# Squares summed on TensorE by pairs of tiles, modulation a tile at a time, and a fixed instruction order at the beginning of a hybrid DeltaNet and neighbourhood-attention layer

## The chip, the cores and the metric

The kernel runs on one core of one Trainium2 chip. The metric is the device time of one execution in microseconds, taken as the median of three runs. The engines are named as in the profile: PE (TensorE, with PEld for its weight loads), DVE (VectorE), ACT (ScalarE), POOL (GpSimd) and SP (SyncE, which here only issues DMAs).

## The reference

One layer over 1024 latent tokens and 256 context tokens, width 1024. The part that the change touches is the very first step: the modulation vectors, the first RMSNorm, and the first column blocks of the input projection.

```python
mod_x = silu(c) @ w_ada + b_ada              # 6 x 1024 columns
mod_c = silu(c_ctx) @ w_ada + b_ada
sh1, sc1, ... = split(mod_x, 6);  csh1, csc1, ... = split(mod_c, 6)
px = (rms_norm(x,   norm1_w) * (1 + sc1)  + sh1)  @ w_in    # 1024 tokens
pc = (rms_norm(ctx, norm1_w) * (1 + csc1) + csh1) @ w_in    #  256 tokens
# rms_norm(x, w) = x * rsqrt(mean(x*x, over the 1024 features) + 1e-6) * w
...
# gated DeltaNet on 2064 columns, neighbourhood attention on 1536,
# output projection, gated residual, second norm, SwiGLU FFN, gated residual
```

## The kernel before

Activations lie transposed: 8 tiles `xt[k]` of 128 features by 1280 tokens (256 context tokens first, then 1024 latent ones). Products are made from float32 split in two parts, high and low, each in the TensorE's reduced form: for each tile `hh[k]` (high) and `hl[k]` (low) of the modulated activations, and `whi`, `wlo` of a weight block, three products are summed: hh with whi, hl with whi, hh with wlo. The 1280 tokens are cut into segments of 256, 512 and 512 columns (`SEGS`), so one block, one tile and one of the three products are three matmuls.

The beginning (lines 624 to 714) runs as follows. SP issues the loads: the 8 tiles of activations (640 KB each), the constants, 1 MB pieces of the modulation weights (`load_ada`, L630), the weights of the first two blocks (`fraw`, L641), six more pieces, and small tables. ACT squares each tile (L680), DVE adds the squares of tiles 0 to 6 into `acc` (L682), and PE multiplies `acc` and the last tile's squares by a matrix of ones (L687), which sums over the features and puts the sum on all partitions. ACT makes rs = exp(-0.5 * ln(mean + eps)) from it (L689 and L690, with a table load ahead of each).

The modulation for the tiles comes in four groups of two tiles. `ada(q)` multiplies the conditioning vectors (`wide`, 32 columns of which 2 count) by two 1 MB pieces (L662, 8 matmuls of 512 columns, each on a 32-row strip of the output), ACT copies the result to SBUF (`arow`, L665), and PE turns the rows into columns with the selector `sel` (L668, 4 matmuls of 2 columns). DVE adds the bias (`mod1`, L671) and makes the scale (`w1s`, L674). Then, for each tile k, DVE multiplies xt by the scale and rs (L701), ACT adds the shift and rounds to `hh` (L702), DVE makes `hl` (L704), each in a context part of 256 and a latent part of 1024 columns, and `b.mm([k])` (L397) issues the nine matmuls of each of the first two blocks. High and low weights of these two blocks are made by ACT (L193) and DVE (L194). Later blocks get their weights from SP's load (L192), ACT (L193) and POOL (L194), and their results are taken out of PSUM by ACT (L430) and run through the short convolution by DVE (L439). L207 loads the remaining modulation weights, which DVE sums in the background (L226, L228).

The order of instructions on each engine isn't the order of the source: a scheduler places each engine's instructions by its own estimate, under the dependences. Buffers come from pools; a buffer's next user waits for its last reader. `ascope` holds the modulation weights (seven buffers of 1 MB) and is closed ahead of tile 4, whose hh and hl reuse that memory.

Of the kernel before, what the change touches and what calls it, by code (L numbers as in the profile page):

```python
# [9 lines left out]
F32 = mybir.dt.float32  # L10
# [3 lines left out]
AF = mybir.ActivationFunctionType  # L14
OP = mybir.AluOpType
AX = mybir.AxisListType
# [4 lines left out]
KT = 8  # L21
# [31 lines left out]
WIN = (256, 0)  # L53
CTX = {256: slice(0, 256), 0: slice(384, 640)}
PACE = 0.72
ORDER = [list(range(NCH)), [1, 0] + list(range(9, 1, -1))]


# [29 lines left out]
def hybrid(ctx, tc, a, dbg):  # L88
# [15 lines left out]
    def lasting(name, shape, dt=F32):  # L104
        return persist.tile(shape, dt, name=name, tag=name)

    prm = lasting("prm", [128, 64])
# [17 lines left out]
    n1w, n2w, bada = prm[:, 0:8], prm[:, 8:16], prm[:, 16:64]  # L125
    cw = const("cw", [128, 12, 5])
    qkw = const("qkw", [128, 2])
    onw = const("onw", [128, 1])
# [52 lines left out]
            dve.scalar_tensor_tensor(r, y, 1.5, r, op0=OP.add, op1=OP.mult)  # L181

    def weights(wp, raws=2):
        def load(src, kt=KT, n=128, lo_engine=pool, raw=None):
# [8 lines left out]
            act.copy(h, r)  # L193
# [175 lines left out]
    with ExitStack() as bs:  # L369
# [13 lines left out]
        hh, hl = [], []  # L383
# [16 lines left out]
        class Block:  # L400
# [7 lines left out]
            def prefetch(self, raw=None, lo_engine=pool):  # L408
# [3 lines left out]
                self.w = load_w(src, lo_engine=lo_engine, raw=raw)  # L412

            def banks(self):
                self.pss = [(bank("blk"), s0, n) for s0, n in self.segs]
# [204 lines left out]
        with ExitStack() as xs:  # L620
            xp = pools(xs, "xp", "left")
            xt = []
            masks = xp.tile([128, 4, 128], F32, name="masks", tag="masks")
            ascope = ExitStack()
            wap = pools(ascope, "wap", "right", 7)
            aw = {}

            def load_ada(j):
                aw[j] = w = wap.tile([128, 4, 512], F32, name="wada", tag="wada")
                sp.dma_start(w, a["wa1"][j // 2, :, 4 * (j % 2):4 * (j % 2) + 4])  # L630

# [12 lines left out]
            sp.dma_start(cw, a["cw"])  # L644
            sp.dma_start(masks, a["masks"])
# [6 lines left out]
            sel = xp.tile([128, 2], F32, name="sel", tag="sel")  # L652
            rs = xp.tile([128, T], F32, name="rs", tag="rs")
            acc = xp.tile([128, T], F32, name="acc", tag="acc")

            def ada(q):

                p = bank("pm")
                for j in (2 * q, 2 * q + 1):
                    w = aw.pop(j)  # L660
                    for k in range(4):
                        pe.matmul(p[32 * k:32 * k + 32], wide[:, 4 * (j % 2) + k], w[:, k], start=j % 2 == 0,  # L662
                                  stop=j % 2 == 1)
                row = xp.tile([128, 512], F32, name="arow", tag="arow", bufs=2)
                act.copy(row, p)  # L665
                p = bank("pm")
                for b in range(4):
                    pe.matmul(p[:, 2 * b:2 * b + 2], row[:, b * 128:(b + 1) * 128], sel, start=True, stop=True)  # L668
                k = slice(2 * q, 2 * q + 2)
                m = mod1.rearrange("p (s b) c -> p s b c", s=2)[:, :, k]  # L670
                dve.tensor_tensor(m, p[:, 0:8].rearrange("p (s b c) -> p s b c", s=2, c=2),  # L671
                                  bada[:, 0:16].rearrange("p (s b c) -> p s b c", s=2, c=1)[:, :, k].to_broadcast(
                                      [128, 2, 2, 2]), OP.add)
                dve.scalar_tensor_tensor(w1s[:, k], m[:, 1], 1.0,  # L674
                                         n1w[:, k].rearrange("p (b c) -> p b c", c=1).to_broadcast([128, 2, 2]),
                                         op0=OP.add, op1=OP.mult)

            for k in range(KT):
                sq = xp.tile([128, T], F32, name="sq", tag="sq", bufs=2)
                act.activation(sq if k else acc, xt[k], AF.Square)  # L680
                if 0 < k < KT - 1:
                    dve.tensor_tensor(acc, acc, sq, OP.add)  # L682
            dve.tensor_reduce(sel, ident.rearrange("p (c i) -> p i c", i=32)[:, 0:2], AX.X, OP.add)
            sums = [bank() for _ in SEGS]
            for i, x in enumerate((acc, sq)):
                for p, (s0, n) in zip(sums, SEGS):
                    pe.matmul(p[:, :n], M[C_ONE], x[:, s0:s0 + n], start=i == 0, stop=i == 1)  # L687
            for p, (s0, n) in zip(sums, SEGS):
                act.activation(rs[:, s0:s0 + n], p[:, :n], AF.Ln, bias=b_eps, scale=1.0 / D)  # L689
            act.activation(rs, rs, AF.Exp, scale=-0.5)  # L690
            ada(0)
            for b, raw in zip(first, raws):
                b.prefetch(raw, dve)
            for k in range(KT):
                if k == 4:
                    ascope.close()
                    h_tiles(pools(bs, "hp2", "right"), 4)
                t = xt[k]
                parts = [(j, x, mod1[:, k, j:j + 1]) for j, x in ((1, slice(0, CT)), (0, slice(CT, T)))]
                for j, x, sh in parts:  # L700
                    dve.scalar_tensor_tensor(t[:, x], t[:, x], w1s[:, k, j:j + 1], rs[:, x], op0=OP.mult, op1=OP.mult)  # L701
                    act.activation(hh[k][:, x], t[:, x], AF.Identity, bias=sh)  # L702
                for j, x, sh in parts:
                    dve.scalar_tensor_tensor(hl[k][:, x], t[:, x], sh, hh[k][:, x].bitcast(F32),  # L704
                                             op0=OP.add, op1=OP.subtract)
                for b in first:
                    b.mm([k])
                if k < 3:
                    ada(k + 1)
                if k == 5:  # L710
                    act.copy(mr[:, 4], ident)
                    for d in range(2):
                        act.mul(mneg[:, d], masks[:, d], -1.0e30)
                    act.copy(mr[:, 0:4], masks)

        cp = pools(bs, "cp", "right")
        late = ExitStack()
# [903 lines left out]
def host(inputs):  # L1621
# [2 lines left out]
    o = {}  # L1624
    o["cst"], o["masks"] = const_arrays()
    o["c2"] = c(np.stack([f("c")[0].reshape(8, 128), f("c_ctx").reshape(8, 128)], -1).transpose(1, 0, 2))
    o["prm"] = c(np.concatenate([f("norm1_w")[0].reshape(8, 128), f("norm2_w")[0].reshape(8, 128),
                                 f("b_ada")[0].reshape(48, 128)], 0).T)
# [59 lines left out]
```

## Time and profile before

| what | value |
|---|---|
| median of 3 runs | 1605.53 us (1604.45 to 1607.15) |
| span of the profiled execution, first to last instruction | 1601.8 us |
| the profiled execution's own time | not recorded beyond the span; the median is 3.7 us above it |
| PE busy | 1509.9 us, 94% of the span |
| DVE busy | 1038.7 us, 65% |
| ACT busy | 706.1 us, 44% |
| POOL busy | 205.5 us, 13% |
| moved by DMA | 271.03 MB, mean 169 GB/s |

The page gives busy times by engine, and cuts the span into 40 slices of 40 us, so the beginning is the first slice and most of the second. The timeline view lists instructions in order of time: start, duration, engine, line, operation, output and inputs, shape, count, and in brackets how long the engine had been idle and what released it. A matmul's duration there includes its way through the array, so that neighbours overlap: the pace of a stream is read from start to start. A product of float32 numbers not split is shown as two rows for one matmul. The windows view gives each engine's busy time in a stretch, the clock that was granted to PE (1.00 is full; stretches for which nothing was recorded also show 1.00), the DMA share and the rate.

### The profile page before, as it was taken

To read this page: it belongs to the slowest core of one execution; us is meant where nothing else is said; L and a number is where in the kernel's file an instruction comes from. 1 tells how busy PE (TensorE), PEld (TensorE's weight loads), DVE (VectorE), ACT (ScalarE), POOL (GpSimd) and SP (SyncE) were. 2 spreads that over 40 slices of the span, in tenths; PEclk is the share of its full clock that TensorE was granted. 3 is DMA by queue.
4 is the path that set the end of the run, shared out by engine and by line. 5 is a ranking of instruction groups with operands and counts; after the bars stand their busy time and mean duration, and the time that the engine had idled before them with its cause. 6 is when DMAs were issued, how large, how long until landed. Compare 5 with 4: busy or idle time off the path is not lost. (4 is left out here: it accounts for less than half of the span.)

```text
span 1601.8 us, 24051 instructions
## 1 busy us (share of the span) xinstructions
PE 1509.9 (94%) x8626; PEld 1269.3 (79%) x8626; DVE 1038.7 (65%) x1934; ACT 706.1 (44%) x1341; POOL 205.5 (13%) x277
## 2 busy tenths in 40 slices
PE   4999999899898897999899999999999999999999
PEld 2788787679788786788777887888888888888887
DVE  4774496674364476667898648956665655679652
ACT  5342554553332325666674347333333333545441
POOL 0054401611333320011110000000000000000000
PEclk8999999999999999999999999999999999999999
DMA  9254222665345538999754910522333333698742
GB/s 387 63 190 133 71 74 78 202 200 178 117 150 184 182 102 228 311 286 288 217 161 135 310 55 27 197 99 99 112 101 107 116 109 109 233 369 299 254 153 85
DMA packets 206407, 271.03 MB, mean 169 GB/s; under 512 B 15952, under 2 KB 115792, under 8 KB 205264
## 3 DMA queue, kind: packets, MB, share of 16 engines
q1 hardware_dynamic: 200816, 264.73, 50.8%
q10 hardware_dynamic: 5472, 4.76, 0.9%
q8 instruction: 68, 1.11, 0.3%
q14 instruction: 51, 0.42, 0.1%
HBM read 204.68 MB, written 68.94 MB: 171 GB/s over the span
## 5 line engine op out<-in xcount | busy, mean ns | idle before, releaser
L397 PE MATMUL blk<-hh,whi 128*128 128x512 f32 (+1 forms) x416 | 125.1, 393 | 4.2 <-ACT hh L702 2.8
L1325 ACT CAST uhi<-ws 128x512 fp32r<-128x512 f32 x91 | 54.7, 622 | 153.8 <-PE ps L1264 75.1
L1325 ACT CAST uhi<-wq 128x512 fp32r<-128x512 f32 x101 | 60.3, 621 | 135.7 <-issue 61.3
L397 PE MATMUL blk<-hh,wlo 128*128 128x512 f32 (+1 forms) x416 | 117.8, 375 | 0.6 <-POOL wlo L194 0.6
L397 PE MATMUL blk<-hl,whi 128*128 128x512 f32 (+1 forms) x416 | 117.5, 374 | 0.0
L1326 DVE TENSOR_TENSOR ulo<-wq,uhi 128x512 fp32r<-128x512 f32 x101 | 67.2, 686 | 66.3 <-ACT uhi L1325 35.4
L1264 PE MATMUL ps<-hT,uhi 128*128 128x512 f32 x336 | 103.9, 390 | 3.1 <-ACT hT L1439 3.1
L1264 PE MATMUL ps<-lT,uhi 128*128 128x512 f32 x336 | 103.9, 391 | 0.0
L1264 PE MATMUL ps<-hT,ulo 128*128 128x512 f32 x336 | 103.8, 390 | 0.0
L1264 PE MATMUL ps<-hB,uhi 128*128 128x512 f32 x288 | 89.7, 392 | 0.0
L1264 PE MATMUL ps<-lB,uhi 128*128 128x512 f32 x288 | 89.2, 391 | 0.0
L1264 PE MATMUL ps<-hB,ulo 128*128 128x512 f32 x288 | 88.9, 389 | 0.0
L397 PEld LDWEIGHTS blk<-hh,whi 128*128 128x128 f32 x416 | 70.8, 194 | 19.7 <-issue 4.9
L397 PEld LDWEIGHTS blk<-hl,whi 128*128 128x128 f32 x416 | 73.5, 192 | 15.2 <-issue 1.7
L397 PEld LDWEIGHTS blk<-hh,wlo 128*128 128x128 f32 x416 | 73.3, 191 | 15.2 <-POOL wlo L194 0.9
L1326 DVE TENSOR_TENSOR ulo<-ws,uhi 128x512 fp32r<-128x512 f32 x91 | 60.7, 685 | 37.7 <-ACT uhi L1325 29.4
L580 PE MATMUL blk<-zhi,hh 128*128 128x256 f32 (+1 forms) x288 | 84.4, 293 | 0.0
L580 PE MATMUL blk<-zhi,hl 128*128 128x256 f32 (+1 forms) x288 | 82.9, 288 | 0.0
L580 PE MATMUL blk<-zlo,hh 128*128 128x256 f32 (+1 forms) x288 | 82.2, 285 | 0.0
L193 ACT CAST whi<-wraw 128x1024 fp32r<-128x1024 f32 x26 | 27.3, 1048 | 112.7 <-PE blk L397 55.7
L1264 PEld LDWEIGHTS ps<-hT,uhi 128*128 128x128 f32 x336 | 62.8, 188 | 16.5 <-ACT hT L1439 3.5
L1264 PEld LDWEIGHTS ps<-hT,ulo 128*128 128x128 f32 x336 | 63.4, 189 | 13.3
(352 smaller groups left out, 3749.0 us busy)
## 6 DMA issues: line engine op xcount, KB each, us to landing
wq<-w_fo SPq DMA_DIRECT2D x99, 256.0 KB
wq<-w_gu SPq DMA_DIRECT2D x88, 256.0 KB
wad<-wa SPq DMA_DIRECT2D x64, 256.0 KB
bt<-rpb SPq DMA_DIRECT2D x64, 192.0 KB
t_d<-g SPq DMA_DIRECT2D x22, 512.0 KB
fr<-t_d SPq DMA_DIRECT2D x44, 256.0 KB
f_d<-g SPq DMA_DIRECT2D x33, 256.0 KB
fr<-f_d SPq DMA_DIRECT2D x33, 256.0 KB
```

The costliest lines, as they stand in the source:

```text
L193: act.copy(h, r)
L397: pe.matmul(o, ww[:, k], xx[k][:, s], start=k == 0 and j == 0, stop=k == KT - 1 and j == 2)
L580: pe.matmul(p[:, :c1 - c0], x[k][:, s], ww[:, k, c0:c1], start=k == 0 and j == 0, stop=k == KT - 1 and j == 2)
L1264: pe.matmul(o, w[wi][:, k], x[xi][:, k], start=first and k == 0 and j == 0, stop=k == n - 1 and j == 2, skip_group_check=True)
L1325: act.copy(hi, self.raw[key])
L1326: dve.tensor_tensor(lo, self.raw[key], hi.bitcast(F32), OP.subtract)
```

## The change

The beginning is rewritten, from the loads to the end of the first two blocks; the later code is the same.

- **Loads**: the first blocks' weights come right behind the activations, then three pieces of modulation weights, the constants and masks, and the other five pieces. A piece now holds, for one tile, the shift and scale columns of all 8 feature groups (still 1 MB).
- **Squares**: ACT squares each tile, DVE adds two neighbouring tiles, and PE multiplies each sum of a pair by the ones as it comes, four times. The last pair goes by segments.
- **Modulation**: `ada(j)` and `column(j)` serve one tile (8 matmuls of 256 columns, 2 matmuls of 2), and stand apart: the table `AHEAD` says behind which tile and block each is issued. The selector comes from the host with `prm`.
- **Weights of the first blocks**: high and low parts of the first on DVE, of the second on POOL.
- **Tile 0** is normed by segments, and its products go in another order (both blocks' hh with whi, both hh with wlo, both hl with whi).
- **Order**: on PE, DVE and ACT this part keeps the order of the source (`manual_schedule`).

```diff
+AHEAD = {(1, 0): (3,), (1, 1): (3, 4), (2, 0): (4, 5), (2, 1): (5, 6, 7), (3, 0): (6, 7)}
...
-            act.copy(h, r)
+            if hi_engine:
+                hi_engine.tensor_copy(h, r)
+            else:
+                act.copy(h, r)
             lo_engine.tensor_tensor(o, r, h.bitcast(F32), OP.subtract)
...
-                aw[j] = w = wap.tile([128, 4, 512], F32, name="wada", tag="wada")
-                sp.dma_start(w, a["wa1"][j // 2, :, 4 * (j % 2):4 * (j % 2) + 4])
+                aw[j] = w = wap.tile([128, KT, 256], F32, name="wada", tag="wada")
+                sp.dma_start(w, a["wa1"][j])
...
-            sp.dma_start(cst, a["cst"])
             raws = [xp.tile([128, KT, 128], F32, name=f"fraw{i}", tag=f"fraw{i}") for i in range(2)]
-            for j in range(2):
-                load_ada(j)
             for i in range(2):
                 sp.dma_start(raws[i], a["w_conv"][4 + i])
-            for j in range(2, 8):
+            for j in range(3):
+                load_ada(j)
+            sp.dma_start(cst, a["cst"])
+            sp.dma_start(masks, a["masks"])
+            for j in range(3, KT):
                 load_ada(j)
...
+            def ada(j, copy):
+                p, w = bank("pm"), aw.pop(j)
+                for k in range(KT):
+                    s = slice(32 * (k % 4), 32 * (k % 4) + 32)
+                    pe.matmul(p[s, :256], wide[:, k], w[:, k], start=k < 4, stop=k >= 4)
+                rows[j] = xp.tile([128, 256], F32, name="arow", tag="arow", bufs=2)
+                copy(rows[j], p[:, :256])
+            def column(j):
+                p, row = bank("pm"), rows.pop(j)
+                for b in range(2):
+                    pe.matmul(p[:, 2 * b:2 * b + 2], row[:, b * 128:(b + 1) * 128], sel, start=True, stop=True)
...
+            with tc.manual_schedule(engines={mybir.EngineType.PE, mybir.EngineType.DVE, mybir.EngineType.Activation}):
+                sums = [bank() for _ in SEGS]
+                segs = [slice(s0, s0 + n) for s0, n in SEGS]
+                for k in range(0, KT, 2):
+                    sq = [xp.tile([128, T], F32, name="sq%d" % i, tag="sq%d" % i, bufs=2 + i) for i in range(2)]
+                    act.activation(sq[0], xt[k], AF.Square)
+                    for s in segs if k == KT - 2 else [slice(0, T)]:
+                        act.activation(sq[1][:, s], xt[k + 1][:, s], AF.Square)
+                        dve.tensor_tensor(sq[1][:, s], sq[0][:, s], sq[1][:, s], OP.add)
+                    for p, s in zip(sums, segs):
+                        pe.matmul(p[:, :s.stop - s.start], M[C_ONE], sq[1][:, s], start=k == 0, stop=k == KT - 2)
+                for p, s in zip(sums, segs):
+                    act.activation(rs[:, s], p[:, :s.stop - s.start], AF.Ln, bias=b_eps, scale=1.0 / D)
+                act.activation(rs, rs, AF.Exp, scale=-0.5)
+                first[0].prefetch(raws[0], dve, dve)
+                first[1].prefetch(raws[1], pool, pool)
+                ada(0, dve.tensor_copy)
+                column(0)
+                normed_tile(0, segs)
+                ada(1, act.copy)
+                for b in first:
+                    b.banks()
+                for j, (w, x) in enumerate(((0, hh), (1, hh), (0, hl))):
+                    for b in first:
+                        for o, s in b.outs:
+                            pe.matmul(o, b.w[w][:, 0], x[0][:, s], start=j == 0, stop=False)
+                        if j == 0 and b is first[1]:
+                            column(1)
+                            normed_tile(1)
+                ada(2, act.copy)
+                column(2)
+                for k in range(1, KT):
+                    if k == 3:
+                        ascope.close()
+                        h_tiles(pools(bs, "hp2", "right"), 4)
+                    if k + 1 < KT:
+                        normed_tile(k + 1)
+                    for j, b in enumerate(first):
+                        b.mm([k])
+                        for q in AHEAD.get((k, j), ()):
+                            if q in rows:
+                                column(q)
+                            else:
+                                ada(q, act.copy)
+                    if k == 5:
...
-    o["wa1"] = c(wada[:, :2048].reshape(8, 128, 2, 4, 256).transpose(3, 1, 0, 2, 4).reshape(4, 128, 8, 512))
+    o["wa1"] = c(wada[:, :2048].reshape(8, 128, 2, 8, 128).transpose(3, 1, 0, 2, 4).reshape(8, 128, 8, 256))
```

Each engine's order in the two built programs was compared. Behind the first two blocks it is the same on all engines but for a few places in the next blocks: PE takes some matmuls of the third and later blocks a few places earlier or later, DVE takes three background sums (L226, L228) behind the first convolution taps instead of ahead of them, and SP issues the next block's weights (L192) ahead of three background loads (L207) instead of behind them.

More of the change, by code (lines that the diff above doesn't have):

```diff
@@ L105, in lasting @@
         return persist.tile(shape, dt, name=name, tag=name)
-    prm = lasting("prm", [128, 64])
+    prm = lasting("prm", [128, 66])
     ones = lasting("ones", [128, 128])
@@ L124, in hybrid @@
     ident = M[C_ID]
-    n1w, n2w, bada = prm[:, 0:8], prm[:, 8:16], prm[:, 16:64]
+    n1w, n2w, bada, sel = prm[:, 0:8], prm[:, 8:16], prm[:, 16:64], prm[:, 64:66]
     cw = const("cw", [128, 12, 5])
@@ L183, in weights, with load @@
     def weights(wp, raws=2):
-        def load(src, kt=KT, n=128, lo_engine=pool, raw=None):
+        def load(src, kt=KT, n=128, lo_engine=pool, raw=None, hi_engine=None):
             given = raw is not None
@@ L651, in hybrid @@
             pool.tensor_copy(wide[:, :, 0:2], sc2)
-            sel = xp.tile([128, 2], F32, name="sel", tag="sel")
             rs = xp.tile([128, T], F32, name="rs", tag="rs")
[L654 to L697, printed above, removed]
+            rows = {}
+            def ada(j, copy):
[5 more added lines that the diff above has]
+                copy(rows[j], p[:, :256])
@@ L698, in hybrid, with normed_tile @@
+            def normed_tile(k, cuts=(slice(0, CT), slice(CT, T))):
                 t = xt[k]
-                parts = [(j, x, mod1[:, k, j:j + 1]) for j, x in ((1, slice(0, CT)), (0, slice(CT, T)))]
-                for j, x, sh in parts:
+                parts = [(x, mod1[:, k, int(x.start < CT):int(x.start < CT) + 1]) for x in cuts]
+                for x, sh in parts:
+                    j = int(x.start < CT)
                     dve.scalar_tensor_tensor(t[:, x], t[:, x], w1s[:, k, j:j + 1], rs[:, x], op0=OP.mult, op1=OP.mult)
@@ L702, in hybrid @@
                     act.activation(hh[k][:, x], t[:, x], AF.Identity, bias=sh)
-                for j, x, sh in parts:
+                for x, sh in parts:
                     dve.scalar_tensor_tensor(hl[k][:, x], t[:, x], sh, hh[k][:, x].bitcast(F32),
                                              op0=OP.add, op1=OP.subtract)
-                for b in first:
[L707 to L714, printed above, removed]
+            with tc.manual_schedule(engines={mybir.EngineType.PE, mybir.EngineType.DVE, mybir.EngineType.Activation}):
[18 more added lines that the diff above has]
+                ada(1, act.copy)
+                for b in first:
+                    b.banks()
[22 more added lines that the diff above has]
+                    if k == 5:
+                        act.copy(mr[:, 4], ident)
+                        for d in range(2):
+                            act.mul(mneg[:, d], masks[:, d], -1.0e30)
+                        act.copy(mr[:, 0:4], masks)
```

13 lines of the change are left out of this document (9 added, 4 removed).

## The prediction

> **What bounds the kernel now.** I read the page first, then the stretches of the beginning, then its timeline and the waits.
>
> ```profile
> span 1601.8 us, 24051 instructions
> ...
> PE   4999999899898897999899999999999999999999
> ...
> PE 39%; DVE 1%; ACT 1%; issue 0%
> ```
>
> The span is PE's: full in nearly all slices, and nearly all of the chain that ended last. That chain covers only 41% of the span, so it doesn't reach back to the beginning, but the row of PE has its one large hole there: slice 1, the first 40 us, is at 4 tenths.
>
> ```profile
> 10.00:15.00 5.00, 0.00 (x0) 0.00 (x0) 4.64 (x4) 3.82 (x3) 0.00 (x0) 1.00 1.02 415
> ...
> 26.00:33.00 7.00, 2.66 (x16) 1.78 (x8) 2.48 (x5) 4.97 (x6) 0.00 (x0) 0.76 1.01 421
> 33.00:40.00 7.00, 5.59 (x13) 3.03 (x13) 6.18 (x8) 2.91 (x4) 0.00 (x0) 0.50 1.02 395
> 40.00:50.00 10.00, 10.00 (x64) 5.93 (x64) 4.85 (x9) 2.90 (x5) 0.00 (x0) 1.00 0.17 41
> ...
> 74.00:100.00 26.00, 25.42 (x144) 21.80 (x143) 20.19 (x31) 14.37 (x22) 10.71 (x5) 1.00 0.45 149
> 100.00:140.00 40.00, 40.00 (x313) 37.98 (x312) 19.58 (x26) 15.93 (x38) 22.53 (x29) 1.00 0.60 191
> ```
>
> Behind each stretch and its length stand the busy times of PE, PEld, DVE, ACT and POOL with their instructions, then PE's clock, the DMA share and GB/s. In the last three rows PE is full but for 0.6 us. Before that it is idle, or (33 to 40) at half clock. Loads run at 415 GB/s.
>
> ```profile
> 7.06 1.27 ACT L680 ACTIVATE sq<-xt 128x1280 f32<-128x1280 f32 x1 [0.17 <-DMA xt<-xcT]
> ...
> 16.60 1.27 ACT L680 ACTIVATE sq<-xt 128x1280 f32<-128x1280 f32 x1 [0.29 <-DMA xt<-xcT]
> ...
> 17.94 4.64 PE L687 MATMUL m<-acc,ones 128*128 128x256 f32 x6 [17.94 <-DVE acc L682]
> ...
> 22.37 2.57 PE L687 MATMUL m<-sq,ones 128*128 128x256 f32 x6
> ...
> 24.87 1.92 PE L662 MATMUL pm<-wada,wide 128*32 128x512 f32 x16
> 24.98 0.69 ACT L689 ACTIVATE rs<-m,bias 128x512 f32<-128x512 f32 x1 [0.17 <-PE m L687]
> 25.56 1.03 ACT L193 CAST whi<-fraw 128x1024 fp32r<-128x1024 f32 x1
> ...
> 26.61 1.28 ACT L690 ACT_TABLE_LOAD   x1
> ...
> 27.91 1.27 ACT L690 ACTIVATE rs<-rs 128x1280 f32<-128x1280 f32 x1
> ...
> 29.70 1.87 PE L668 MATMUL pm<-sel,arow 128*128 128x2 f32 x8 [2.91 <-ACT arow L665]
> ...
> 32.60 0.51 ACT L702 ACTIVATE hh<-xt,mod 128x256 fp32r<-128x256 f32 x1 [2.00 <-DVE xt L701]
> 33.16 0.58 PE L397 MATMUL blk<-hh,whi 128*128 128x256 f32 x1 [1.59 <-ACT hh L702]
> ```
>
> This is the chain of the beginning: last tile at 16.6, sums on PE, logarithm, exponential (done at 29.18), modulation of the first tiles, first product at 33.16.
>
> ```profile
> 74.21 0.75 PE L397 MATMUL blk<-hl,whi 128*128 128x256 f32 x3
> ...
> 74.79 0.75 PE L397 MATMUL blk<-hh,wlo 128*128 128x256 f32 x3
> ...
> 75.38 0.51 PE L397 MATMUL blk<-hh,whi 128*128 128x256 f32 x2
> ```
>
> Three matmuls of 256, 512 and 512 columns take 0.585 us from start to start, and at 75.38 groups of two begin: the third block. So the first two blocks end at **75.38**, and the question is when they end now.
>
> **The change, step 1: rs.** The sum moves under the loads. Pair one can be added when the second tile is squared (7.06 + 1.27 = 8.33).
>
> ```profile
> L682 DVE TENSOR_TENSOR acc<-acc,sq 128x1280 f32<-128x1280 f32 x6 | 8.9, 1492 | 7.9 <-ACT sq L680 7.5
> ```
>
> Adding takes 1.49, so PE starts at about 9.9. It now sums four times instead of twice. The same three matmuls took 22.37 - 17.94 = 4.43 us from rest and 24.87 - 22.37 = 2.50 after that, so I take 4.43 + 3 x 2.50 = 11.9: done at 21.8 instead of 24.87. The last third of the last pair is there at about 19.1 (16.60, 1.7 for squaring in three cuts, 0.7 for the last addition), before PE asks for it at 19.3, so PE sets this, not the loads. Then ACT: 0.1 to start, 0.69, table load 1.28, exponential 1.27: rs at **25.2** instead of 29.18. The rounding of weights that stood in between (1.03) goes to DVE and POOL.
>
> **Step 2: the first product.** Before, 3.98 us lay between rs and it (copy of the row, the 1.87 for the selector, bias and scale, xt, hh). Now tile 0's columns are made ahead of rs. Its piece lands at about 21.7 (16.6, then twice 0.5 MB and 1 MB at 415 GB/s); `ada(0)` is half of 1.92, the copy some 0.4 by DVE, the selector half of 1.87, bias and scale 0.4: 24.6, just under the cover of ACT's exponential. If a load is 1 us late, 0.4 of it shows. What remains is xt (0.48) and hh (0.51) and the crossings: first product at **26.3**, 6.9 earlier. This half of the gain is nearly certain if step 1 holds.
>
> **Step 3: the two blocks.** PE's own floor: 8 tiles x 2 blocks x 3 products x 0.585 = 28.1; `ada` 1 to 7, one of which lies ahead of 26.3, is 6 x 0.96 = 5.8; seven `column` calls.
>
> ```profile
> 44.61 1.01 PE L668 MATMUL pm<-sel,arow 128*128 128x2 f32 x8
> ...
> 45.66 0.17 DVE L671 TENSOR_TENSOR mod<-pm,prm 128x8 f32<-128x8 f32 x1 [5.08 <-PE pm L668]
> 45.85 0.16 DVE L674 SCALAR_TENSOR_TENSOR w1s<-mod,prm 128x4 f32<-128x4 f32 x1
> ```
>
> Four selector matmuls take 1.01 at full clock, so two take 0.5, seven times 3.5: 26.3 + 28.1 + 5.8 + 3.5 = 63.7. Both kinds are the same total work as before, cut finer; DVE's small operations double (0.4 us for each tile with the hand-overs). But in source order DVE is slower than that.
>
> ```profile
> 65.44 1.68 DVE L701 SCALAR_TENSOR_TENSOR xt<-xt,w1s,rs 128x256 f32<-128x256 f32 x2
> ...
> 67.03 0.48 DVE L704 SCALAR_TENSOR_TENSOR hl<-xt,mod,hh 128x256 fp32r<-128x256 f32 x1
> 67.15 1.15 ACT L702 ACTIVATE hh<-xt,mod 128x1024 fp32r<-128x1024 f32 x1 [0.69 <-DVE xt L701]
> ...
> 68.33 1.29 DVE L704 SCALAR_TENSOR_TENSOR hl<-xt,mod,hh 128x1024 fp32r<-128x1024 f32 x1 [0.82 <-ACT hh L702]
> ```
>
> This is one tile on its own: xt, xt, hl, a wait of 0.82 for ACT, hl, 4.1 us until DVE can begin the next. The scheduler filled that wait with the next tile's xt; the fixed order can't, and pays it eight times. DVE then needs 25.2 + 8 x 4.1 + 7 x 0.4 = 60.8. To this come waits for the columns of tiles 1 and 2, which are not issued ahead: ACT copies their rows only behind hh of the tile before, and PE has products of both blocks queued in front. Tile 1's row is copied at about 28.3 and its column made at about 29.8, while DVE is free at 28.7 (25.2 and 3.5 for tile 0), with bias and scale a wait of 1.5; tile 2's comes up to 1 late in the same way. So the last hl is ready at 63.3, and five of PE's six products of tile 7 (2.9) follow it: **66.2**. Masks and constants on ACT (1.5 us between tiles 6 and 7) lie in DVE's time. At full clock throughout the waits for columns shrink by 1.7: 64.5. If PE runs from 26 to 33 us at half clock, as it did from 33 to 40 before, it does 3.3 us less in that time: 67.8. I take 66.3: 75.4 - 66.3 = **9.1 us**.
>
> Half clock is the point to weigh. The windows above grant 0.50 from 33 to 40, although PE worked in most of it, after a stretch (26 to 33) with 2.66 busy of 7. The new beginning has such a stretch too, from the sums' end to about 30. The Trainium skill ("TensorE: Matmul & The Clock Gate", Part 1) says that PE's clock is halved after a window of some 3.4 us with little work and restored after a busy one. The rows agree as to both directions. By that rule the result would be the 67.8 (7.6 us gained), inside my range.
>
> The second block's weights now pass through POOL beside DVE's work.
>
> ```profile
> 88.81 2.46 POOL L573 TENSOR_TENSOR zlo<-wraw,zhi 128x1056 fp32r<-128x1056 f32 x1 [4.58 <-DVE acc L228]
> ...
> 89.38 3.23 DVE L228 SCALAR_TENSOR_TENSOR acc<-wad,sc,acc 128x512 f32<-128x512 f32 x2
> ```
>
> The first of these two DVE operations begins inside POOL's and the pair takes 3.23, though neither waited for data: a DVE operation can be held up by a whole POOL one. The weights land at 19.1; a copy of at most 2.5 and a subtraction of 2.46, taking turns with DVE's two, end at about 24.5, ahead of xt at 25.2. If they collide, up to 2.4 us are lost; I take 0. The Trainium skill ("SBUF — State Buffer", "Who interferes with whom") gives the reason, a port pair that DVE and POOL take turns on; this row agrees.
>
> **Step 4: does the gain reach the end?** The instruction order behind the two blocks is the same but for a few neighbours.
>
> ```profile
> PE pr L928 <- DVE y L938: 7.2, 4, 4.0
> PE pr L928 <- DVE kk L919: 6.9, 11, 2.1
> PE sc L296 <- DVE mx L298: 5.7, 5, 4.2
> ...
> SPq L207 <- ACT mr L714: 20.4, 1, 20.4
> ```
>
> PE's later waits are for DVE, ACT and POOL, whose work hangs on the same blocks; the first later load waits for ACT's copy of the masks, which moves forward too. The three background sums that DVE did in its idle time before the first convolution (2 us) now stand between its taps; PE is behind with other blocks then, so 0, at most 2. I carry all 9.1 over: span 1592.7, and with the 3.7 us by which the median stands above the span, **1596.4**, said as 1596.5.
>
> **The rivals.**
>
> *Cold sums.* Every pair at 4.43: rs 5.8 later, and the end at 72.1: 1602.2. For it: PE pauses between pairs once it is fast. Against: each sum at the slow pace is longer than the loads of a pair (3.2 us), so PE doesn't pause while it is slow; in the old trace the pace rose under just this work.
>
> *Given back later.* The beginning is 9 us shorter, but the blocks behind meet something that didn't move (a load, POOL's backlog) or more half-clock stretches: 1604, no difference. Against: PE is full from 74 to 140, and no load stands at the top of PE's waits.
>
> *Columns in line (slower).* In fixed order a tile's path may close into a ring: `ada` 0.96, row copy 0.4, selector 0.5, bias and scale 0.4, DVE's 4.1 and hand-overs, 6.6 a tile instead of 4.5, more at half clock (another 0.5). It decides if tiles 3 to 7 wait for their columns as I let 1 and 2. Then seven times 2.1 to 2.6, less the 2.5 counted, are 12 to 16 us on 66.3: 78.5 to 82, some 3 to 7 us behind the old 75.4: about 1610. Against: columns 3 to 7 are issued one to three tiles ahead.
>
> *Better.* Full clock, no waits for columns: PE's floor 63.7 or slightly less: 1593.
>
> **How the numbers follow.** 0.2%, about what a measurement of this kernel can tell from no change, is 3.2 us: faster is below 1602.3, slower above 1608.7. Chances: forecast (1594 to 1599.5) 0.68, better 0.07, cold sums 0.10 (half of it counted as faster), given back 0.09, columns in line 0.06. So faster 0.80, same 0.14, slower 0.06. The range 1593.0 to 1602.5 holds the forecast, most of the better case and the cold sums.
>
> **What would show it.** The new trace should have sums from 9.9 to 21 or 22, the exponential's end near 25, the first product near 26.3, groups of two (third block) near 66, DVE with waits of 0.8 for ACT in each tile 3 to 7, and no PE wait for a column from tile 3 on. I am wrong if rs comes after 27, if the third block starts after 70, or if it starts at 66 and the end doesn't move by about as much.

## The result and the profile after

The changed kernel takes **1618.68 us** (median of 4 runs, 1615.66 to 1619.54) against 1605.84 for the kernel before beside it: ratio **1.0074**, 95% interval 1.0060 to 1.0088. It is 12.8 us slower, where 9 us faster was forecast. The profiled execution has a span of 1617.0 us against 1601.8.

The page of the changed kernel, the rows that answer to those of before:

```profile
span 1617.0 us, 24224 instructions
...
PE   6999898999888898999899999999999999999999
...
PE 40%; DVE 1%; ACT 1%; issue 0%
```

The hole of the first 40 us is partly filled (6 tenths instead of 4), and PE is full elsewhere, as before. The stretches of the beginning, with the columns as before (PE, PEld, DVE, ACT, POOL, clock, DMA share, GB/s):

```profile
10.00:15.00 5.00, 4.79 (x7) 2.52 (x8) 1.75 (x3) 4.03 (x4) 0.00 (x0) 1.00 1.02 423
26.00:33.00 7.00, 6.29 (x18) 4.94 (x19) 5.29 (x10) 2.83 (x6) 0.00 (x0) 0.53 1.03 431
33.00:40.00 7.00, 6.51 (x56) 4.15 (x55) 4.09 (x8) 3.13 (x5) 0.00 (x0) 0.99 0.98 382
40.00:50.00 10.00, 10.00 (x101) 7.14 (x100) 6.94 (x13) 2.68 (x5) 0.00 (x0) 1.00 0.16 42
74.00:100.00 26.00, 26.00 (x152) 22.58 (x151) 20.82 (x33) 13.11 (x19) 13.43 (x10) 1.00 0.58 192
100.00:140.00 40.00, 38.07 (x311) 36.58 (x310) 16.34 (x24) 16.84 (x42) 17.88 (x23) 1.00 0.62 197
```

PE works from 10 us on, and the half clock lies at 26 to 33 us instead of 30 to 40. From the timeline of the changed kernel, the sums, the exponential, the first product and the first group of two (the third block):

```profile
10.21 11.78 PE L700 MATMUL m<-sq,ones 128*128 128x256 f32 x24 [10.21 <-DVE sq L698]
...
24.03 1.27 ACT L703 ACTIVATE rs<-rs 128x1280 f32<-128x1280 f32 x1
...
26.42 0.58 PE L715 MATMUL blk<-hh,whi 128*128 128x256 f32 x1 [1.21 <-ACT hh L685]
...
69.07 0.51 PE L401 MATMUL blk<-hh,whi 128*128 128x256 f32 x2
```

So rs is done at 25.30 (before 29.18), the first product comes at 26.42 (33.16) and the third block at 69.07 (75.38). The beginning did gain, 6.3 us here. To see where it went, I paired each matmul with the same one of before and took the difference of their starts: -6.9 us at 70, -5.4 at 200, -3.5 at 510, 0.0 from 700 to 900, **+0.6 at 1000 and +14.9 at 1590**. Two losses, then: 7.5 us between 70 and 1000, in steps, and 14.3 us at an even rate from 1000 on, in the FFN, which the change does not touch. The windows show that second one. Before, then after:

```profile
1000.00:1300.00 300.00, 300.00 (x1332) 248.62 (x1331) 191.60 (x304) 106.99 (x193) 0.00 (x0) 1.00 0.35 117
```

```profile
1000.00:1300.00 300.00, 300.00 (x1296) 242.60 (x1295) 187.68 (x297) 104.93 (x189) 0.00 (x0) 1.00 0.33 115
```

PE is busy without a gap in both and has its full clock, but it gets through 36 matmuls fewer in 300 us. No wait, no DMA, no clock: each matmul takes longer. The timeline, before and after:

```profile
1200.18 0.62 PE L1264 MATMUL ps<-hB,uhi 128*128 128x512 f32 x2
1200.63 0.62 PE L1264 MATMUL ps<-lB,uhi 128*128 128x512 f32 x2
...
1202.45 0.61 PE L1264 MATMUL ps<-hT,ulo 128*128 128x512 f32 x2
1202.90 0.62 PE L1264 MATMUL ps<-hT,uhi 128*128 128x512 f32 x2
```

```profile
1200.40 0.63 PE L1288 MATMUL ps<-hT,uhi 128*128 128x512 f32 x2
1200.87 0.63 PE L1288 MATMUL ps<-lT,uhi 128*128 128x512 f32 x2
...
1203.19 0.61 PE L1288 MATMUL ps<-hB,uhi 128*128 128x512 f32 x2
1203.64 0.62 PE L1288 MATMUL ps<-lB,uhi 128*128 128x512 f32 x2
```

From start to start a pair takes 0.45 us before, 0.47 after with `hT`; and in the changed kernel some pairs with `hB` still take 0.45. Over single matmuls the median is 227 ns before and 234 to 235 after for `hT` and `lT`. An engine that is 100% busy in both profiles hides this: only a count, or start to start, shows it.

What differs is one line of the diff that the section on the change mentions in a clause (the selector comes from the host with `prm`):

```diff
-    prm = lasting("prm", [128, 64])
+    prm = lasting("prm", [128, 66])
```

`prm` is the first tile of the left-side memory, and its 256 bytes a partition become 288 with padding, so every later left-side tile stands 32 bytes further on. Tiles allocated from the right side don't move. In the FFN the weights `uhi`, `ulo` are left tiles, of the moving operands only `hB11` and `lB11` are; `hT`, `lT` and the other `hB`, `lB` are right ones. In the compiled programs (bytes in a partition):

```
                       before  changed  prm 80  pad 64
uhi   (weights)         24800    24832   24864   25056
hB11  (moving, left)    49632    49664   49696   49888
hT1   (moving, right)  180192   180192  180192  180192
uhi - hT1, modulo 256       0       32      64       0
```

Of the FFN's 2796 matmuls of 512 columns (2795 intervals from start to start), 2268 have their distance changed; the 528 with `hB11` and `lB11` keep it, and those are the pairs that still take 0.45 us. In this one execution the mean from start to start is 227.4 ns over the matmuls that stand at distance 0 and 233.3 over those at 32. The kernel has pads in front of the FFN's pools (`shift(ctx, "pad", "left", 8)`, L1249 of before), with which all of them stand at distance 0 before.

### The profile page after: what moved, and what is told of

Read it like the earlier page. It is cut to its first block, busy times and chain, and to the rows that moved or that the text cites. A ratio compares the mean times of both kernels' runs of the same rounds, so it can differ in the third digit from the quotient of the medians.

```text
span 1617.0 us, 24224 instructions
## 1 busy us (share of the span) xinstructions
PE 1531.6 (95%) x8702; PEld 1275.3 (79%) x8702; DVE 1037.6 (64%) x1944; ACT 704.8 (44%) x1345; POOL 209.8 (13%) x279
## 5 line engine op out<-in xcount | busy, mean ns | idle before, releaser
L1350 DVE TENSOR_TENSOR ulo<-wq,uhi 128x512 fp32r<-128x512 f32 x101 | 67.3, 689 | 68.3 <-PE ps L1631 29.9
L1288 PEld LDWEIGHTS ps<-lT,uhi 128*128 128x128 f32 x336 | 63.4, 189 | 15.4
```

Source lines behind the costliest of these rows:

```text
L1288: pe.matmul(o, w[wi][:, k], x[xi][:, k], start=first and k == 0 and j == 0, stop=k == n - 1 and j == 2, skip_group_check=True)
L1350: dve.tensor_tensor(lo, self.raw[key], hi.bitcast(F32), OP.subtract)
```

## The experiments

**Theory**: the distance between weights and moving operand sets the pace of the FFN's matmuls, and the 32 bytes cost the 14 us. **Rivals**: the new order, the clock, or the DMA makes the FFN slow; or the loss is the half clock's.

### The 32 bytes alone, in the old kernel

```diff
-    prm = lasting("prm", [128, 64])
+    prm = lasting("prm", [128, 72])
-    act.dma_start(prm, a["prm"])
+    act.dma_start(prm[:, 0:64], a["prm"])
```

> The kernel before the change with nothing but prm 72 columns wide instead of 64 (the load fills the first 64): the 32-byte shift alone, with the old beginning. Address theory: the FFN pace goes from 227 to 234 ns and the time from 1605.8 to 1619-1621, slower than the changed kernel by about the 0 to 6 us that its beginning gains. Rival (order or clock): nothing changes, 1605-1607.

Measured: 1621.36 us, ratio 1.0109 (1.0089 to 1.0128) to the kernel before; 16.3 us slower with not one instruction of the computation changed. The median pace of the `hT` products is 234 ns, and the same matmul falls behind by 14.3 us from 1000 to 1590, as in the changed kernel. That shows the cause of the larger loss; order and beginning are not needed for it.

### 64 bytes instead of 32, in two ways

```diff
-    prm = lasting("prm", [128, 66])
+    prm = lasting("prm", [128, 80])
-    act.dma_start(prm, a["prm"])
+    act.dma_start(prm[:, 0:66], a["prm"])
```

> The changed kernel with prm 80 columns wide instead of 66 (the load fills the first 66), so that every later tile of the left-side pools moves by another 32 bytes and stands in 64-byte steps where it stood before the change. Address theory: the FFN's 512-column matmuls go back from 234 to 227 ns start to start; over some 2,900 of them that is about 14 to 18 us, and the time falls from 1618.7 to 1600-1605. Rival (the slower FFN comes from the new order or the clock): pace stays at 234 and the time at 1617-1620. A third possibility: the pace hangs on 128- or 256-byte steps, which this does not restore; then too it stays at 1617-1620.

```diff
-    shift(ctx, "pad", "left", 8)
+    shift(ctx, "pad", "left", 16)
```

> The changed kernel with prm left at 66 columns and the left-side pad ahead of the FFN's pools 16 instead of 8 wide: only the FFN's left tiles are moved by 32 bytes, those of the blocks before it stay shifted. Address theory: FFN pace 227 ns, time 1600-1605; if the slow loss of the gain between 250 and 680 us comes from the shift as well, this one is 4-6 us slower than the kernel with prm 80 wide; if that loss comes from half-clock stretches, the two agree within 2 us. Rival (order or clock): 1617-1620.

Measured: 1613.92 (ratio 1.0058, 1.0043 to 1.0073) and 1614.15 (1.0054, 1.0039 to 1.0069). The pace stays at 233 ns and the loss from 1000 to 1590 at 14.4 and 14.3 us. My first guess, steps of 64 bytes, fell. The two agree within 0.3 us, so it makes no difference whether the tiles ahead of the FFN stand 64 bytes further on (the first) or 32 (the second). What 32 against 0 does there is seen in two runs of the old kernel: from 80 to 1000 us the one with `prm` 72 wide, whose tiles are moved there, falls 3.5 us behind the first profile of before, and the one with the pad 56 wide (below), whose tiles are not, 2.9 us. So the addresses cost little ahead of the FFN, as far as single profiles show it.

### The distance by itself

A program of nothing but 512-column matmuls in groups of 12, with the start of the weights moved by 32 bytes from group to group, for five starts of the moving operand. It leaves out the whole computation.

> A program of nothing but 512-column fp32r matmuls (it leaves out the whole computation and writes one product as output): groups of 12 with two weight tiles in turn, a group for each of 17 starts of the weights, 32 bytes apart, and 5 starts of the moving operand (0, 32, 64, 128, 256 bytes on); finer steps of 8 bytes; and groups with one weight tile for two matmuls, as in the blocks. Address theory: groups come at 227 or 234 ns start to start, and which of them is decided by the distance of weights and moving operand within 128 bytes (0 is fast) or within 256. Rival 1: each operand's own start decides (one row or one column of the table is fast throughout). Rival 2: all groups are alike at one pace, and the pace in the whole kernels hangs on something that this program does not have (DMA, other engines' reading).

Each entry is the mean of ten intervals from start to start within a group, in ns; the columns are the weights' start, the rows the moving operand's:

```
bytes      0    32    64    96   128   160   192   224   256
  0    226.6 233.1 233.3 234.0 231.7 233.8 229.2 233.1 226.6
 64    229.0 233.2 226.7 233.1 233.3 234.0 231.6 233.7 229.2
128    231.7 233.7 229.2 233.1 226.6 233.1 233.3 234.0 231.7
256    226.6 233.1 233.3 234.0 231.7 233.8 229.2 233.1 226.6
```

Each row is the one above, moved along: for starts that are multiples of 32 bytes neither operand's own start counts, only weights minus moving operand, modulo 256 bytes. 0 is fast, 192 costs 2.6 ns, 128 costs 5.1, the others 6.5 to 7.4. The row for 32 bytes follows it too, but for its first group at distance 0, which came at 229.0: there the single intervals are 235, 225, 230, 236, 229, 232, 231, and 227 only from the eighth on. With one weight tile for two matmuls in turn the values are the same, but for such a first group at each start (230.5 and 228.9). Finer steps of the weights, with the moving operand at 0, give 230.7 ns at 8 bytes and 233.2 at 16. With the moving operand itself at 16 bytes the rule does not hold: the weights at 16 too (distance 0) give 231.1, and the least, 228.4, comes with the weights at 48. All this was measured in one execution. There is no DMA and no other engine's work in that stretch, so those rivals are out.

### The table used on the whole kernel: 192 bytes, and back to 0

```diff
-    shift(ctx, "pad", "left", 8)
+    shift(ctx, "pad", "left", 56)
```

This edit is made in the kernel before:

> The kernel before the change with that pad 56 instead of 8 wide, 192 bytes: the FFN's weights then begin 192 bytes (modulo 256) from the moving operands for 2268 of the 2795 matmuls. The table of offsets gives 229.2 ns there, 2.6 more than at 0: 2268 x 2.6 = 5.9 us, 1611. If only in line or not in line counts (a step, not the table's values), as with prm 72 wide: 1619-1621. If the distance doesn't matter: 1605.

Measured: 1612.09, ratio 1.0031 (1.0018 to 1.0043), 5.4 us slower where the table gave 5.9; the same matmul loses 5.6 us from 1000 to 1590. It is the table's value, not a step.

```diff
-    shift(ctx, "pad", "left", 8)
+    shift(ctx, "pad", "left", 64)
```

This one is made in the changed kernel (32 and 224 more bytes make 256):

> The changed kernel with the left-side pad ahead of the FFN's pools 64 instead of 8 wide: with prm's 32 bytes that makes 256, so weights and moving operands of the FFN begin a multiple of 256 bytes apart again, as in the kernel before; nothing ahead of the FFN changes. Address theory by the table of offsets (226.6 ns at distance 0, 233.1 to 233.4 at 32 and 64): 2268 of the FFN's 2795 matmuls lose 6.5 to 7.5 ns each, 15 to 17 us: from 1618.7 to 1602-1604, and to 1598-1600 if its front part goes as in the kernels with prm 80 and pad 16 (1614). Rival (the slower FFN comes from the order): 1614-1619, pace 233-235 ns.

Measured: **1602.0**, ratio **0.9965** (0.9952 to 0.9978): faster than before. Its window counts again what before had:

```profile
1000.00:1300.00 300.00, 300.00 (x1332) 248.77 (x1332) 192.71 (x306) 107.15 (x193) 0.00 (x0) 1.00 0.35 117
```

The loss from 1000 to 1590 is 0.0 us. That settles it from both sides: the 32 bytes alone slow the old kernel down, and 224 more bytes of pad cure the changed one. Why the chip minds this distance, no run shows.

### The changed kernel again, and free order

> The changed kernel as it is, once more, beside the others on this chip. It came out at 1618.7 and the kernels with prm 80 and with pad 16, of the same FFN pace, at 1614: 4.6 us apart. If that is what differs between executions (more half-clock stretches in that one), this one comes at 1613-1616; if 32 bytes are dearer than 64 bytes in the blocks ahead of the FFN, again at 1618-1619.

Measured: 1616.12 (1610.08 to 1619.14), ratio 1.0055 (1.0037 to 1.0072): neither of the two expected bands alone, but a spread over both. This execution's profile has a span of 1608.3 against 1617.0 of the first, with the same instructions. The beginning differs by the clock. The first profile of the changed kernel, then this one:

```profile
24.00:34.00 10.00, 8.49 (x40) 6.07 (x39) 6.52 (x14) 5.10 (x8) 0.00 (x0) 0.66 1.02 423
```

```profile
24.00:34.00 10.00, 8.44 (x59) 5.69 (x51) 8.48 (x16) 4.69 (x8) 0.00 (x0) 1.00 1.01 419
```

and the third block comes 3.9 us earlier:

```profile
65.13 0.52 PE L401 MATMUL blk<-hh,whi 128*128 128x256 f32 x2
```

Then the beginning without the fixed order, first with `prm` 80 wide, then with the pad 64 wide:

```diff
-            with tc.manual_schedule(engines={mybir.EngineType.PE, mybir.EngineType.DVE, mybir.EngineType.Activation}):
+            if True:
```

> The kernel with prm 80 wide, and the beginning without the fixed source order (the scheduler orders PE, DVE and ACT there as elsewhere). By step 3 of the prediction the fixed order costs DVE a wait of about 0.8 us in each of eight tiles; if the scheduler fills it, the third block begins 3 to 6 us earlier than 69.1 (63 to 66) and the end moves by as much or less. If the order is no matter, the third block begins at 69 and the time is that of the kernel with prm 80 wide; if the scheduler puts bulk work or columns in the way, later than 70.

> The changed kernel with that pad 64 wide and the beginning in the scheduler's order instead of source order. By the earlier pair the order is worth 0 to 1 us: 1598-1603, within 1.5 us of the kernel with the pad alone. If the fixed order of the beginning cost what step 3 of the prediction says (0.8 us for each of eight tiles), 4 to 6 us less than with the pad alone.

Measured: 1612.9 (ratio 1.0050, 1.0035 to 1.0065) beside 1613.9 with the fixed order, and **1600.36** (0.9960, 0.9947 to 0.9973) beside 1602.0. The third block begins at 66.89 beside 67.26, and at 66.36 beside 67.00: 0.4 to 0.6 us, not 4 to 6. Even that is not the order's: in the clock records of the beginning, free order has 3.4 us of half clock beside 6.8, and none beside 6.8. Where the half clock is alike, the fixed order is ahead, by 1.2 and 1.0 us with one profile each. Without any, the third block begins at 65.13 in fixed order (above) and here in free order at

```profile
66.36 0.52 PE L401 MATMUL blk<-hh,whi 128*128 128x256 f32 x2
```

With 6.8 us from 26.4 on, it begins at 69.07 in fixed order (the first profile) and at 70.09 in free order, in the last run below:

```profile
70.09 0.51 PE L401 MATMUL blk<-hh,whi 128*128 128x256 f32 x2
```

The difference in time, 1.0 and 1.6, lies within the intervals.

### The two parts of the beginning

The new sums alone in the kernel before (its `acc` and two sums replaced by the four sums of pairs of the diff), and the new modulation alone in the changed kernel with pad 64 (the old sums put back):

> The kernel before with the new sums alone: squares summed on PE by pairs of tiles as they land, the old modulation and order, prm and the FFN's addresses as they were. By steps 1 and 2 of the prediction rs comes 4 us earlier and takes the first product along by 2 to 4; if the old modulation hid none of it the third block begins 3 to 4 us earlier than 75.4 (71.4 to 72.4) and the end is at 1602-1603. Rival: the old path then waits for the modulation's own loads and matmuls, the third block moves by less than 1.5 us and the end not at all (1605-1607), so that the gain needs both parts.

> The changed kernel with the pad 64 wide (FFN in line again) and the old sums: squares added up on DVE, two sums on PE at the end; the new modulation by tile in fixed order stays. rs then comes at about 29 again instead of 25; the first product follows at 30 to 31, and the third block begins at 71 to 72 if the modulation by tile is worth the other 4 us (time 1602-1605), at 67 to 68 if it alone carries the gain (time 1600-1602), at 75 if the gain comes from the sums (1606).

Measured: sums alone 1604.56, ratio 0.9985 (0.9976 to 0.9994).

```profile
23.60 1.27 ACT L690 ACTIVATE rs<-rs 128x1280 f32<-128x1280 f32 x1
...
28.44 0.58 PE L397 MATMUL blk<-hh,whi 128*128 128x256 f32 x1 [1.59 <-ACT hh L702]
...
74.23 0.52 PE L397 MATMUL blk<-hh,whi 128*128 128x256 f32 x2
```

rs is done at 24.87, but the first product waits until 28.44 and the third block until 74.23, 1.2 us earlier than before: the rival, the old modulation is in the way. Not quite as the rival had it, 0.15% of the time is gained, just clear of nothing. Modulation alone 1605.15, ratio 0.9998 (0.9988 to 1.0009).

```profile
26.39 1.27 ACT L704 ACTIVATE rs<-rs 128x1280 f32<-128x1280 f32 x1
...
28.78 0.58 PE L716 MATMUL blk<-hh,whi 128*128 128x256 f32 x1 [1.27 <-ACT hh L685]
...
71.26 0.51 PE L401 MATMUL blk<-hh,whi 128*128 128x256 f32 x2
```

rs is done at 27.66, ahead of the 29 that I expected: the rounding of weights (1.03 us of ACT before) no longer stands between logarithm and exponential, and the last logarithm starts 0.6 us earlier (24.39 against 24.98). The first product is at 28.78 and the third block at 71.26, 4.1 us earlier, of which nothing can be measured at the end. Together (pad 64) the third block is 8.4 us earlier and the time 0.35% less (0.22 to 0.48%). So each part alone gives less than both. That they give more together than their sum (0.15 and 0.02%) is not shown: the intervals are too wide for it.

### Short matmuls in line

```diff
-                self.hi = self.zp().tile([128, KT, 264], F32R, name="zhi", tag="zhi")
+                self.hi = self.zp().tile([128, KT, 320], F32R, name="zhi", tag="zhi")
...
+        shift(late, "zpad", "left", 24)
```

(`zlo` likewise.)

> The changed kernel with the pad 64 wide and free order in the beginning, and besides the tiles zhi and zlo 320 instead of 264 columns wide with 96 bytes of pad ahead, so that the 864 matmuls of 256 and 264 columns of the gate and value products also have weights and moving operands a multiple of 256 bytes apart (now they are at all distances). If the table of offsets holds for matmuls of half the length, they go from 118-122 ns to 113-117, some 4 us less than the 1600.4 without it: 1595-1598. If only the long ones gain (or the lock is lost at each of these shorter matmuls), the same pace and 1599-1602.

Measured: 1600.69, ratio 0.9965 (0.9953 to 0.9978), no gain over the 1600.36. The two are from different chips, and this run's third block came 3.7 us later than that one's (70.09 against 66.36), so the times alone could hide a gain of that size. The pace decides: the medians of these matmuls were 118 to 121 ns and are 120 in line. In the kernel before, where they stand at all eight distances, 256 columns have a median of 120 ns at distance 0 and of 117 to 120 at the others. So the table doesn't hold for 256 and 264 columns in this stream; why was not tried.

## Why the prediction was wrong, step by step

**What bounds the kernel** stands: PE is the span before and after.

**Steps 1 and 2** were right: rs at 25.30 (forecast 25.2), first product at 26.42 (26.3). The sums run from 10.2 to 22.0, the rival of cold sums did not come, and POOL's and DVE's collision on the first weights cost nothing, as I took it.

**Step 3** had the size roughly, and the waits that it named, but not what they are worth. Forecast 66.3, with 64.5 for full clock and 67.8 for half clock from 26 to 33; the third block came at 69.07 in the first profile, at 65.13 in the execution without half clock, and at 67.0 to 67.3 in the kernels with pad 64, pad 16 and `prm` 80. DVE of the changed kernel in its first tiles:

```profile
30.51 0.16 DVE L674 TENSOR_TENSOR mod<-pm,prm 128x4 f32<-128x4 f32 x1 [1.64 <-PE pm L672]
...
36.35 0.16 DVE L674 TENSOR_TENSOR mod<-pm,prm 128x4 f32<-128x4 f32 x1 [1.19 <-PE pm L672]
...
41.51 0.16 DVE L674 TENSOR_TENSOR mod<-pm,prm 128x4 f32<-128x4 f32 x1 [0.51 <-PE pm L672]
...
44.87 1.28 DVE L687 SCALAR_TENSOR_TENSOR hl<-xt,mod,hh 128x1024 fp32r<-128x1024 f32 x1 [0.82 <-ACT hh L685]
...
48.08 0.16 DVE L674 TENSOR_TENSOR mod<-pm,prm 128x4 f32<-128x4 f32 x1 [1.59 <-PE pm L672]
48.28 0.23 DVE L677 TENSOR_SCALAR w1s<-mod,prm 128x2 f32<-128x2 f32 x1
48.41 1.68 DVE L684 SCALAR_TENSOR_TENSOR xt<-xt,w1s,rs 128x256 f32<-128x256 f32 x2
```

The waits of 0.82 for ACT and those for columns 1 and 2 (1.64 and 1.19; forecast 1.5 and up to 1) are there. But the forecast had no wait for a column from tile 3 on, and there are two: 0.51 for column 3, and 1.59 for column 5, which stands ahead of tile 4's xt in the fixed order, though tile 4 does not need it. What was off is the weight of DVE's path. It was to set the time, 2.5 us behind PE's own floor; but PE has work queued through nearly all of these waits, in the changed kernel:

```profile
34.00:68.00 34.00, 33.18 (x242) 25.45 (x242) 23.20 (x38) 14.04 (x25) 0.00 (x0) 1.00 0.30 102
```

and once the products of tile 0 are under way it waits for DVE a single time, for the last tile:

```profile
66.17 0.73 PE L401 MATMUL blk<-hl,whi 128*128 128x512 f32 x2 [0.33 <-DVE hl L687]
```

That fits the free order, which gained nothing at the same clock.

**Step 4 failed.** It said that the instruction order behind the two blocks is the same but for a few neighbours, which holds, and from that carried all 9.1 us to the end, with 0 to 2 us for anything behind the beginning. Two things were missing.

The larger one is no instruction at all: **the width of `prm`**, an edit to which the prediction gave no term. It moves the left-side tiles by 32 bytes and costs 14.3 us in the FFN. The table accounts for it: 2268 matmuls at 233.1 instead of 226.6 ns are 14.7 us. The trace of before could not have given the price, since all of the FFN's matmuls there are at distance 0; but the pads in the code, and an allocation order that puts `prm` first, were a sign that positions matter, and a comparison of addresses would have shown the shift.

The smaller one is that the end shows less than the third block. With the pad 64 wide, 0.35% is left (0.22 to 0.48%), 5.6 us, of the 8.4 us at the third block. How much of that is really given back is less sure, because the 8.4 sets one profile against one, and the half clock of the beginning moves the third block. The old beginning has it at 75.38 in the profile of before, and at 73.74 and 72.92 in those with `prm` 72 wide and with pad 56; the new one in fixed order has it from 65.13 to 69.07 in five profiles. The means are 74.0 and 67.1, which are 6.9 apart.

One piece that is given back shows in the windows: from 100 to 140 us PE was busy for 40.00 us, and now for 38.07 (38.22 with the pad 64 wide). The waits of PE from 66 to 140 us, in the changed kernel with pad 64:

```profile
PE blk L401 <- ACT kk L546: 1.4, 1, 1.4
PE blk L401 <- POOL wlo L198: 0.6, 1, 0.6
PE blk L584 <- ACT kk L546: 0.4, 1, 0.4
```

Of these, before had only the wait for POOL. The 1.8 us for ACT are the prediction's rival "given back later": PE comes earlier to work for which ACT isn't ready yet. For the rest I took the same work in each profile, between the matmuls that before has at 80 and at 1000 us. It takes the kernel with pad 64 8.9 us longer. PE is idle for 4.8 us more of it (68.6 against 63.8), the 1.8 among them. Half clock covers 6.8 us more (51.2 against 44.4); counting only where PE was busy, at half speed, that costs 2.8 us. The remaining 1.4 I can't place. Part of this is scatter between executions: the old kernel with pad 56, which is the kernel before up to the FFN, has the same 44.4 us of half clock there and yet takes 2.9 us longer than before, idle for 3.1 us more.

Here are the sum of the half-clock stretches up to 1560 us in each profile's clock record, and where the same matmul at 1000 us stands against before (whose sum is 54.6; minus is earlier). They go together only loosely:

```
kernel                      half clock, us   at 1000 us
changed, second profile               37.5         -8.2
pad 64, free order                    41.0         -7.6
prm 80, free order                    44.4         -2.7
prm 80                                47.8         -5.3
pad 16                                47.8         -4.7
pad 64, wide tiles in line            47.8         -3.1
changed, first profile                58.0         +0.6
pad 64                                58.0         +0.9
```

The two profiles of the changed kernel, whose instructions are the same, differ by 20.5 us of half clock and by 8.8 us at 1000 us; half of 20.5 is 10.3, so half clock is enough to explain these two. The stretches come as 3.4, 6.8 or 10.2 us, mostly from 250 to 700 us, where PE waits often, and which waits are followed by one changes from execution to execution. The Trainium skill ("TensorE: Matmul & The Clock Gate", Part 1) describes a clock that is halved or restored by how busy a window of some 3.4 us was; the lengths agree. That the place of these windows against the program decides is a guess, not shown: nothing here could set it.

**The range** (1593.0 to 1602.5) does not hold the changed kernel: no rival had a mechanism by which the FFN's matmuls become slower. It holds the changed kernel with the FFN back in line, 1602.0, but only at its slow end, between the forecast of 1596.5 and the 1604 of "given back later". So the forecast of 9.1 us would have been too high even then: 5.6 us were gained, 3.5 to 7.7 by the interval.

## What to carry to other kernels

A change's cost is not confined to the instructions that it touches: a tile that grows moves every tile allocated behind it. So compare the addresses, not only the order, and where a stage that was not touched becomes slower at an even rate with its engine 100% busy, count its instructions in a fixed window and look at where its operands lie. Pad what grows to a multiple of 256 bytes, as the 224 more bytes did here, so that the distance of weights and moving operand in the hottest 512-column matmuls stays 0 modulo 256. And where two orders are compared by one profile each, compare their half clock first: here it moved the third block by 3.9 us with the same instructions.

## What the hardware showed that I had not expected

- A stream of 512-column fp32r matmuls, each with new weights, runs at 226.6 ns when weights and moving operand start a multiple of 256 bytes apart, at 229.2 at 192 bytes, at 231.7 at 128, and at 233.1 to 234.0 at the others (starts in steps of 32 bytes). It isn't always instantaneous: three groups at distance 0 took seven to nine intervals to come down to 227.
- The products of the blocks (L397), with 256, 512 and 512 columns in turn, are at distance 0 for most of their matmuls as well, and still have a median of 231 to 233 ns for 512 columns. Shorter matmuls in the stream may keep it from settling, which was not tried apart.
- The same program differed by 8.7 us in span between two executions, with 20.5 us more of half clock.
